# Two-layer fp32 trunk on one core: P.V key blocks in both column halves of TensorE, one-step pre-norm scaling, another order of attention steps

## The chip, the cores and the metric

One core of one Trainium2 chip runs the whole program in one launch. The metric is the device time of an execution in microseconds (us), and the kernel before is given as the median of three runs.

## The reference, cut to what matters

The trunk has two layers on 256 tokens of 1024 columns. Layer 0 is half SwiGLU, causal pooling mixer, half SwiGLU; layer 1 has sparse attention in the place of the pooling. Every sub-layer norms its input and its output.

```python
def rms_norm(x, g):
    y = xf * lax.rsqrt(jnp.mean(xf * xf, axis=-1, keepdims=True) + EPS)
    return (y * g.astype(jnp.float32)).astype(x.dtype)
...
    for i in range(DEPTH):
        g = norm_gains[i]
        f = swiglu(rms_norm(x, g[0]), ffn_w_gate[i, 0], ffn_w_up[i, 0], ffn_w_down[i, 0])
        x = x + 0.5 * rms_norm(f, g[1])
        h = rms_norm(x, g[2])
        m = pool_mixer(...) if i % N_MIXERS == 0 else nsa_mixer(...)
        x = x + rms_norm(m, g[3])
        f = swiglu(rms_norm(x, g[4]), ffn_w_gate[i, 1], ffn_w_up[i, 1], ffn_w_down[i, 1])
        x = x + 0.5 * rms_norm(f, g[5])
...
    # nsa_mixer: 16 heads in 4 key/value groups, head size 64
    o = gts[:, :, 0] * o_cmp + gts[:, :, 1] * o_sel + gts[:, :, 2] * o_win
    return o.reshape(B, S, Q_WIDTH) @ w_o
```

At 256 tokens the selected blocks and the window both cover all earlier keys, so the kernel computes the selected and the window branch as two dense causal branches of softmax(QK)V, and the compressed branch on 15 pooled keys.

## The kernel before, in words

Weights come from HBM in pieces of 128x1024 fp32 into a ring of four buffers (`raw`, issued by SP). ScalarE rounds each piece to fp32r (`hi`, the line `nc.scalar.activation(hi...)` in `pieces_of`), VectorE subtracts to get the rest (`lo`), and TensorE multiplies hi.hi, lo.hi and hi.lo into one sum (`mm3`). Tokens are worked in two tiles t of 128. An instruction scheduler orders the program for each engine; `urgent`, `after` and the attention's list `NSA_STEPS` guide it.

Between sub-layers, `post` adds the normed output to x, and `Pre.emit` makes the next input: `scaled` multiplies x by the gain (first 512 columns on POOL, L358, the others on VectorE, L359), `rstd` squares and sums x on ScalarE (L338), adds the halves on VectorE (`ms`, L341) and takes the power -0.5 on POOL (`rs`, L343). Where the input is normed at once, VectorE multiplies by that factor (L396, two halves), and TensorE transposes the result (L366). The pooling mixer applies the factor later.

In the attention, `qk(t, g)` makes the scores of a key/value group on TensorE (L850, L852), the row maximum on VectorE (L854), the exponentials on ScalarE (L856), the reciprocal and the gate product on VectorE (L861, L864), and POOL scales the weights (L865). `pv(t, g)` takes the key blocks (branch and key tile) in twos: TensorE transposes the weights of a block (L881), ScalarE copies the first block to SBUF and VectorE the second, and TensorE multiplies each by V in plain fp32 (L891). V has 64 columns, so the first block of the two uses the left half of TensorE's columns and the second the right half:

```python
nc.tensor.matmul(of32[i * HD:(i + 1) * HD], V[:, kt, br, g], PT[i], start=n == 0, stop=False)
```

The compressed branch adds two products with VC of 256 columns each, one in each half (L898). As both halves of the output are partial sums of the same four heads, ScalarE copies one (L909) and VectorE adds it to the other (L911) before the result is split in hi and lo. `cmp_mm` (L740) is the product of the compressed keys with its weights, also in both halves; `out_proj` is the last product of the attention, `wo` its weights.

Of the kernel before, what the change touches and what calls it, by code (L numbers as in the profile page):

```python
# [9 lines left out]
F32 = mybir.dt.float32  # L10
# [7 lines left out]
P = 128  # L18
# [20 lines left out]
    ("load", 1, 0),  # L39
    ("cpost", 0, 0),  # L40
    ("load", 1, 1),
    ("proj", 0, 1),
    ("load", 4, 0),
    ("proj", 1, 0),
    ("load", 4, 1),
    ("wcmp", 0, 0),
    ("proj", 4, 1),
    ("proj", 4, 0),
    ("load", 3, 0),
    ("cpost", 0, 1),  # L50
    ("proj", 1, 1),
    ("kpost", 0, 1),
    ("load", 3, 1),
    ("cmp", 0, 0),
    ("cpost", 1, 0),
    ("proj", 3, 0),
    ("hid", 0, 0),
    ("cpost", 1, 1),
    ("proj", 3, 1),
    ("kcmp", 0, 0),  # L60
    ("q", 0, 0),
    ("nope", 0, 0),
    ("wcmp", 1, 0),
    ("gates", 0, 0),
    ("vpost", 0, 1),
    ("load", 5, 0),
    ("cmp", 1, 0),
    ("q", 0, 1),
    ("load", 5, 1),
    ("vpost", 0, 0),  # L70
    ("rope", 0, 0),
    ("pc", 0, 0),
    ("proj", 5, 0),
    ("nope", 0, 1),
    ("hid", 1, 0),
    ("vcmp", 0, 0),
    ("pc", 0, 1),
    ("pct", 0, 0),
    ("rope", 0, 1),
    ("proj", 5, 1),  # L80
    ("q", 1, 0),
    ("qk", 0, 1),
    ("qk", 0, 0),
    ("nope", 1, 0),
    ("qk", 0, 1),
    ("qk", 0, 0),
    ("qk", 0, 0),
    ("q", 1, 1),
    ("pct", 0, 1),
    ("qk", 0, 0),  # L90
    ("nope", 1, 1),
    ("qk", 0, 1),
    ("rope", 1, 0),
    ("pv", 0, 0),
    ("qk", 0, 1),
    ("pv", 0, 0),
    ("pv", 0, 0),
    ("pc", 1, 0),
    ("qk", 1, 0),
    ("pv", 0, 1),  # L100
    ("pv", 0, 1),
    ("pv", 0, 1),
    ("vcmp", 1, 0),
    ("pct", 1, 0),
    ("qk", 1, 0),
    ("qk", 1, 0),
    ("qk", 1, 0),
    ("pv", 1, 0),
    ("pv", 1, 0),
    ("pv", 1, 0),  # L110
    ("pv", 1, 0),
    ("qk", 1, 1),
    ("qk", 1, 1),
    ("pv", 1, 0),
    ("rope", 1, 1),
    ("qk", 1, 1),
    ("qk", 1, 1),
    ("pv", 1, 1),
# [50 lines left out]
def _const_arrays():  # L169
# [14 lines left out]
    sel = np.repeat(np.eye(4, dtype=np.float32), P, axis=1)  # L184
# [8 lines left out]
    return np.ascontiguousarray(small), band, np.ascontiguousarray(sel)  # L193
# [13 lines left out]
def _layout(x, norm_gains, ffn_w_gate, ffn_w_up, ffn_w_down, pool_w, pool_b, pool_scale,  # L207
# [12 lines left out]
    a["pbs"] = np.ascontiguousarray(np.concatenate([pool_b[0].reshape(4, 256), pool_scale[0].reshape(4, 256)], axis=1))  # L220
# [13 lines left out]
    a["c_small"], a["c_band"], a["c_sel"] = _const_arrays()  # L234
# [4 lines left out]
def _trunk(ctx: ExitStack, tc: tile.TileContext, d, out):  # L239
# [44 lines left out]
    def piece(src, pool=None, tag="w", bufs=3, step=1024, cut=1024):  # L284
        return pieces_of(raw_piece(src, cut), pool, tag, bufs, step)

    def pieces_of(raw, pool=None, tag="w", bufs=3, step=1024):
# [35 lines left out]
    def halves(v):  # L323
        return [v[:, H[h]] for h in range(2)]
# [715 lines left out]
```

## Time and profile before

| | |
|---|---|
| median of 3 runs | 948.96 us (948.4 to 949.82) |
| the profiled execution's own time | 950.01 us |
| its span | 948.2 us |
| TensorE busy | 928.3 us, 98% of the span |
| VectorE, ScalarE, POOL busy | 655.1, 470.3, 78.8 us |

The span is the stretch from the first to the last instruction that the profiler saw; what the time has above it lies around the program. PE is TensorE, PEld its weight load, DVE VectorE, ACT ScalarE, SP the engine that issues the loads. A plain fp32 matmul leaves two records in the trace, an fp32r one leaves one. Records of matmuls overlap, so what one costs TensorE is read from its start to the start of the next.

### The profile page before, as it was taken

What the parts mean: (1) busy time and instruction counts of PE and PEld (TensorE: products, weight loads), DVE (VectorE), ACT (ScalarE), POOL (GpSimd) and SP (SyncE); (2) the same over time, 40 slices, a digit from 0 to 9 for tenths busy, and PEclk for the clock granted to TensorE, in tenths of its full rate; (3) what the DMA queues carried; (4) which work ended last, traced back from release to release, by engine and by line L of the source; (5) the groups of instructions that cost most, each with busy time, mean ns of one, the idle gap of its engine ahead of it and who ended that gap; (6) DMA issues with size and microseconds to landing.
All of it is one profiled execution on the core that took longest, in us unless ns stands there. A gap on an engine that the chain in (4) does not pass through costs nothing.

```text
span 948.2 us, 13030 instructions
## 1 busy us (share of the span) xinstructions
PE 928.3 (98%) x4882; PEld 769.6 (81%) x4882; DVE 655.1 (69%) x961; ACT 470.3 (50%) x800; POOL 78.8 (8%) x70
## 2 busy tenths in 40 slices
PE   8999999999999999999999999999999999999997
PEld 5888888877888888878888888888655678888886
DVE  6857577786967666658676676777974668676653
ACT  7644445355744344446444443546953566544421
POOL 1000001131000000120000002000542130000000
PEclk9999999999999999999999999999999999999999
DMA  8866675335866566248665652852200358665611
GB/s 321 288 206 199 213 239 196 116 107 168 281 218 220 180 195 205 89 148 279 218 208 190 200 182 78 315 200 90 90 0 24 110 179 285 207 217 182 196 45 44
DMA packets 48033, 168.96 MB, mean 178 GB/s; under 512 B 5593, under 2 KB 6105, under 8 KB 47970
## 3 DMA queue, kind: packets, MB, share of 16 engines
q1 hardware_dynamic: 47970, 168.13, 53.3%
q8 instruction: 38, 0.62, 0.3%
q14 instruction: 25, 0.20, 0.1%
HBM read 167.06 MB, written 1.05 MB: 177 GB/s over the span
## 4 chain that ended last, share of the span: by engine, by line
PE 51%; DVE 4%; ACT 2%; POOL 1%; issue 1%; DVEq 0%; POOLq 0%; ACTq 0%
PE g L503 14%; PE g L504 7%; PE acc L306 5%; PE acc L308 5%; PE acc L307 5%; PE g L306 3%; PE g L308 3%; PE g L307 3%; PE g L891 2%; PE g L881 1%; PE g L471 1%; POOL fx L358 1%; ACT big L856 1%; DVE ast L854 1%; DVE wlo L297 1%
## 5 line engine op out<-in xcount | busy, mean ns | idle before, releaser
L503 PE MATMUL g<-xT,whi 128*128 128x512 f32 x1152 | 406.0, 394 | 0.0
L504 PE MATMUL g<-xT,wlo 128*128 128x256 f32 x1152 | 325.1, 282 | 0.0
L296 ACT ACTIVATE whi<-raw 128x1024 fp32r<-128x1024 f32 (+2 forms) x252 | 205.1, 862 | 151.9 <-issue 48.3
L297 DVE TENSOR_TENSOR wlo<-raw,whi 128x1024 fp32r<-128x1024 f32 (+2 forms) x252 | 242.3, 1003 | 44.3 <-ACT whi L296 43.8
L503 PEld LDWEIGHTS g<-xT,whi 128*128 128x128 f32 x1152 | 216.3, 188 | 49.6
L504 PEld LDWEIGHTS g<-xT,wlo 128*128 128x128 f32 x1152 | 216.5, 188 | 1.4
L297 DVE TENSOR_TENSOR dlo<-raw,dhi 128x1024 fp32r<-128x1024 f32 (+1 forms) x128 | 119.2, 954 | 105.0 <-ACT dhi L296 104.7
L296 ACT ACTIVATE dhi<-raw 128x1024 fp32r<-128x1024 f32 (+1 forms) x128 | 103.8, 842 | 158.0 <-DMA raw<-in_wd 151.7
L440 DVE TENSOR_REDUCE sg<-g 128x256 f32<-128x512 f32 x144 | 97.8, 686 | 56.1 <-PE g L504 55.7
L306 PE MATMUL acc<-dhi,hTh 128*128 128x512 f32 x288 | 112.3, 390 | 0.0
L307 PE MATMUL acc<-dlo,hTh 128*128 128x512 f32 x288 | 112.0, 389 | 0.0
L308 PE MATMUL acc<-dhi,hTl 128*128 128x512 f32 x288 | 111.5, 389 | 0.0
L306 PE MATMUL g<-whi,xT 128*128 128x512 f32 (+2 forms) x168 | 63.9, 384 | 0.8 <-ACT xT L311 0.7
L307 PE MATMUL g<-wlo,xT 128*128 128x512 f32 (+2 forms) x168 | 63.8, 380 | 0.5 <-DVE wlo L297 0.5
L308 PE MATMUL g<-whi,xT 128*128 128x512 f32 (+2 forms) x168 | 63.5, 379 | 0.0
L343 POOL TENSOR_TENSOR rs<-ms,neghalf 128x1 f32<-128x1 f32 x24 | 13.6, 565 | 598.4 <-DVE ms L341 598.4
L306 PEld LDWEIGHTS acc<-dhi,hTh 128*128 128x128 f32 x288 | 54.1, 188 | 11.3
L308 PEld LDWEIGHTS acc<-dhi,hTl 128*128 128x128 f32 x288 | 54.0, 188 | 11.3
L307 PEld LDWEIGHTS acc<-dlo,hTh 128*128 128x128 f32 x288 | 54.1, 188 | 9.9
L306 PEld LDWEIGHTS g<-whi,xT 128*128 128x128 f32 x168 | 31.9, 191 | 7.5 <-ACT xT L311 2.0
L307 PEld LDWEIGHTS g<-wlo,xT 128*128 128x128 f32 x168 | 32.0, 190 | 7.1 <-DVE wlo L297 1.3
L308 PEld LDWEIGHTS g<-whi,xT 128*128 128x128 f32 x168 | 31.9, 190 | 6.4 <-DVE xT L312 0.7
(176 smaller groups left out, 991.4 us busy)
## 6 DMA issues: line engine op xcount, KB each, us to landing
raw<-in_wu SPq DMA_DIRECT2D x88, 512.0 KB, 4.6
raw<-in_wd SPq DMA_DIRECT2D x88, 512.0 KB, 4.5
raw<-in_wg SPq DMA_DIRECT2D x86, 512.0 KB, 3.9
raw<-in_win SPq DMA_DIRECT2D x18, 512.0 KB, 4.3
gain<-in_gains SPq DMA_DIRECT2D x11, 512.0 KB, 3.7
raw<-in_wo SPq DMA_DIRECT2D x8, 512.0 KB, 4.8
big<-in_wk SPq DMA_DIRECT2D x4, 512.0 KB, 5.9
big<-in_wv SPq DMA_DIRECT2D x4, 512.0 KB, 9.3
```

The costliest lines, as they stand in the source:

```text
L296: nc.scalar.activation(hi[:, n + a:n + b], r[:, a:b], AF.Copy)
L297: nc.vector.tensor_tensor(lo[:, n + a:n + b], r[:, a:b], hi[:, n + a:n + b].bitcast(F32), op=OP.subtract)
L306: nc.tensor.matmul(o, A[0], B[0], start=start, stop=False)
L307: nc.tensor.matmul(o, A[0], B[1], start=False, stop=False)
L308: return nc.tensor.matmul(o, A[1], B[0], start=False, stop=stop)
L343: nc.gpsimd.tensor_tensor(r, v, neghalf, op=OP.pow)
L358: nc.gpsimd.tensor_tensor(xg[:, H[0]], x[t][:, H[0]], g[:, H[0]], op=OP.mult)
L440: nc.vector.tensor_reduce(dst, o.rearrange("p a b -> p b a"), axis=AX.X, op=OP.add)
L471: nc.tensor.matmul(o, A(t, k)[i], B[k][j], start=n == 0, stop=n == len(its) - 1)
L503: nc.tensor.matmul(o, hi, pre.xx[:, :, k, :], start=k == 0, stop=False)
L504: nc.tensor.matmul(o[:, 1, :], lo, xT[0][:, k, :], start=False, stop=k == KD - 1)
L891: nc.tensor.matmul(of32[i * HD:(i + 1) * HD], V[:, kt, br, g], PT[i], start=n == 0, stop=False)
```

## The change: what it does

- `pv`: a key block is multiplied by V in two matmuls of 256 columns, one into each column half, as the compressed branch was. The halves of the output are then different heads, and the copy and the two adds (L909, L911) go.
- `Pre.emit`: a normed input takes x, the row's factor and the gain in one VectorE operation for each half. The pooling mixer's input takes its gain product on VectorE alone.
- The gate products (`ar`, `cst`), the scaling of the compressed weights (`ce`) and the `lo` part of the `wo` weights move from VectorE to POOL.
- The pooling's bias is one row of 1024 columns, added by 8 matmuls of 512 columns in the place of 16 of 256; its values come through two of the `raw` buffers.
- `NSA_STEPS` has the same kinds of steps in another order.

```diff
     def scaled(t, g):
         xg = fx[t]
-        nc.gpsimd.tensor_tensor(xg[:, H[0]], x[t][:, H[0]], g[:, H[0]], op=OP.mult)
-        nc.vector.tensor_mul(xg[:, H[1]], x[t][:, H[1]], g[:, H[1]])
+        for h in range(2):
+            nc.vector.tensor_mul(xg[:, H[h]], x[t][:, H[h]], g[:, H[h]])
...
+                elif self.normed:
+                    self.r[t] = r = rstd(halves(x[t]), False, t)
+                    xg = fx[t]
+                    for h in range(2):
+                        nc.vector.scalar_tensor_tensor(xg[:, H[h]], x[t][:, H[h]], r, self.g[:, H[h]], op0=OP.mult, op1=OP.mult)
                 else:
                     xg = scaled(t, self.g)
                     self.r[t] = r = rstd(halves(x[t]), False, t)
-                if self.normed and self.n:
-                    for h in range(2):
-                        nc.vector.tensor_scalar(xg[:, H[h]], xg[:, H[h]], r, None, op0=OP.mult)
...
+        for h in range(2):
+            bs = pp.tile([P, 1024], F32, name="raw", bufs=4)
+            nc.sync.dma_start(bs[0:1], d["pbs"][:, h * 1024:(h + 1) * 1024])
...
+            nc.gpsimd.tensor_tensor(bs[:, 0], bs[:, 0], bs[:, 1], op=OP.mult)
+            nc.gpsimd.tensor_copy(bias[0][:, H[h]], bs[:, 0])
+            nc.gpsimd.tensor_tensor(bias[1][:, H[h]], bs[:, 0], bias[0][:, H[h]].bitcast(F32), op=OP.subtract)
...
-                nc.vector.tensor_mul(st[:, 1], st[:, 1], gates[t][:, 8 * c:8 * c + 8])
-                nc.vector.tensor_mul(e, e, bc(st[:, 1]))
+                nc.gpsimd.tensor_tensor(st[:, 1], st[:, 1], gates[t][:, 8 * c:8 * c + 8], op=OP.mult)
+                nc.gpsimd.tensor_tensor(e, e, bc(st[:, 1]), op=OP.mult)
...
-                    nc.vector.tensor_mul(rv, rv, gv)
+                    nc.gpsimd.tensor_tensor(rv, rv, gv, op=OP.mult)
...
-                o = psG.tile([P, 2, 2, P], F32, name="g")
...
+                o = psG.tile([P, 2, P], F32, name="g")
+
+                def mm(A, B, start, stop):
+                    for par in range(2):
+                        nc.tensor.matmul(o[par * HD:(par + 1) * HD].rearrange("p b q -> p (b q)"), A,
+                                         B[:, par].rearrange("p b q -> p (b q)"), start=start, stop=stop)
...
-                        nc.tensor.matmul(of32[i * HD:(i + 1) * HD], V[:, kt, br, g], PT[i], start=n == 0, stop=False)
+                        mm(V[:, kt, br, g], qs_[i], n == i == 0, False)
...
-                for i in range(2):
-                    nc.tensor.matmul(o[i * HD:(i + 1) * HD, i].rearrange("p b q -> p (b q)"), VC[c],
-                                     q[:, i].rearrange("p b q -> p (b q)"), start=False, stop=True)
+                mm(VC[c], q, False, True)
...
-                ol = np_.tile([P, 512], F32, name="y", bufs=3)
-                of = np_.tile([P, 2, P], F32, name="of", bufs=1)
-                ol = ol[:HD].rearrange("p (a b q) -> p a b q", a=2, b=2)
-                nc.scalar.activation(ol, o[HD:], AF.Copy)
-                for par in range(2):
-                    nc.vector.tensor_tensor(of[par * HD:(par + 1) * HD], o[:HD, par], ol[:, par], op=OP.add)
-                split([v[:, 2 * g:2 * g + 2, :] for v in OT[t]], of)
+                split([v[:, 2 * g:2 * g + 2, :] for v in OT[t]], o)
...
-                    wo.append(ksplit(piece(d["wo"][:, i * 2048:(i + 1) * 2048], step=512), 2))
+                    wo.append(ksplit(piece(d["wo"][:, i * 2048:(i + 1) * 2048], step=512, eng=nc.gpsimd), 2))
```

Where the order of instructions moves, it is shown as the built programs have it. Line numbers of the change differ from those of before by a few. First TensorE in the middle of the attention: V products, transposes of weights (`big`) and of queries (`q`), and products with VC. Before:

```order
L798 MATMUL g<-csm,q_6161 128x128 x4
L891 MATMUL g<-PT,V 64x512
L798 MATMUL g<-csm,q_6161 128x128 x4
L891 MATMUL g<-PT,V 64x512
L881 MATMUL g<-csm,big 128x128 x4
L898 MATMUL g<-PT,VC_5108 64x256 x2
L881 MATMUL g<-csm,big 128x128 x4
```

The change, at the same place (L880 are the products with V and VC, L893 and L803 the transposes):

```order
L880 MATMUL g<-PT,V 64x256 x4
L893 MATMUL g<-csm,big 128x128 x8
L880 MATMUL g<-PT,VC_5094 64x256 x2
L803 MATMUL g<-csm,q_6163 128x128 x4
L880 MATMUL g<-PT,V 64x256 x2
L803 MATMUL g<-csm,q_6163 128x128 x4
L880 MATMUL g<-PT,V 64x256 x2
L774 MATMUL g<-wv_5088,rep 128x64 x2
L893 MATMUL g<-csm,big 128x128 x4
```

A V product of 512 columns often stands by itself before; in the change the two 256-column products of a block stand next to each other everywhere. Next POOL, from the second scaling of softmax weights on. Before, scalings follow each other:

```order
L343 TENSOR_TENSOR rs_5169<-ms_5167,neghalf 128x1
L865 TENSOR_TENSOR big<-big,ar 128x4x128 x4
L865 TENSOR_TENSOR big<-big,ar 128x1024
L895 TENSOR_TENSOR PT<-Pc,csm 128x512
L865 TENSOR_TENSOR big<-big,ar 128x1024
L895 TENSOR_TENSOR PT<-Pc,csm 128x512
```

The change (L870 are the scalings, L296 the `lo` parts of `wo`, L825 and L826 the compressed weights, L869 the gate products):

```order
L870 TENSOR_TENSOR big<-big,ar 128x4x128
L296 TENSOR_TENSOR wlo<-raw,whi 128x512
L825 TENSOR_TENSOR cst<-cst,gates_5079 128x8
L296 TENSOR_TENSOR wlo<-raw,whi 128x512 x3
L826 TENSOR_TENSOR ce<-ce,cst 128x128
L296 TENSOR_TENSOR wlo<-raw,whi 128x512 x4
L869 TENSOR_TENSOR ar<-ar,gates_5078 128x4
L870 TENSOR_TENSOR big<-big,ar 128x4x128
L869 TENSOR_TENSOR ar<-ar,gates_5079 128x4
L870 TENSOR_TENSOR big<-big,ar 128x1024
L906 TENSOR_TENSOR PT<-Pc,csm 128x512
```

Between the second and the third scaling now stand eight `wo` pieces and three small products. Last TensorE ahead of the attention, at `cmp_mm` of the compressed keys (the tile `big` here is its data; L696 and L707 are transposes). Before, its 32 matmuls stand in one row:

```order
L308 MATMUL g<-whi,xT 128x512
L696 MATMUL g<-csm,fx_70 128x128 x4
L740 MATMUL g<-big 64x128 x32
L707 MATMUL g<-csm,y 128x128 x4
L306 MATMUL g<-whi,xT 128x512
```

The change, where L745 is `cmp_mm` and L305 to L307 are the three products of `mm3`:

```order
L307 MATMUL g<-whi,xT 128x304
L745 MATMUL g<-big 64x128 x11
L305 MATMUL g<-whi,xT 128x512
L745 MATMUL g<-big 64x128 x8
L306 MATMUL g<-wlo,xT 128x512
L307 MATMUL g<-whi,xT 128x512
L305 MATMUL g<-whi,xT 128x512
L306 MATMUL g<-wlo,xT 128x512
L307 MATMUL g<-whi,xT 128x512
L305 MATMUL g<-whi,xT 128x512
L745 MATMUL g<-big 64x128 x4
```

The one row has become four, of 11, 8, 4 and (behind these) 9 matmuls, with other products between them.

## Rows read from the trace of the kernel before

**Rows 1.** The page's part 1: busy us (share of span) and instructions.

```profile
PE 928.3 (98%) x4882; PEld 769.6 (81%) x4882; DVE 655.1 (69%) x961; ACT 470.3 (50%) x800; POOL 78.8 (8%) x70
```

**Rows 2.** Part 4, the chain that ended last, by engine.

```profile
PE 51%; DVE 4%; ACT 2%; POOL 1%; issue 1%; DVEq 0%; POOLq 0%; ACTq 0%
```

**Rows 3.** Windows: stretch, length, busy PE, PEld, DVE, ACT, POOL; clock, DMA share, GB/s.

```profile
0.00:596.00 596.00, 590.30 (x3043) 499.63 (x3044) 417.75 (x546) 293.35 (x433) 34.92 (x38) 1.00 0.60 198
650.00:690.00 40.00, 36.65 (x216) 28.17 (x215) 35.29 (x105) 31.80 (x122) 15.49 (x12) 1.00 0.18 61
690.00:745.00 55.00, 53.82 (x247) 31.96 (x245) 30.09 (x65) 24.23 (x71) 18.79 (x15) 0.97 0.06 20
```

**Rows 4.** Timeline, PE: start, length, operation, records [idle before]; first and last lone V product.

```profile
677.01 1.07 PE L891 MATMUL g<-PT,V 128*64 128x512 f32 x2
...
734.98 1.07 PE L891 MATMUL g<-PT,V 128*64 128x512 f32 x2
735.98 0.50 PE L306 MATMUL acc<-whi,xT 128*128 128x512 f32 x1
```

**Rows 5.** Timeline, PE: two V products in a row; a VC pair and what follows.

```profile
711.43 1.08 PE L891 MATMUL g<-PT,V 128*64 128x512 f32 x4
712.34 0.60 PE L898 MATMUL g<-PT,VC 128*64 128x256 f32 x4
...
718.88 0.65 PE L898 MATMUL g<-PT,VC 128*64 128x256 f32 x4
719.46 0.66 PE L881 MATMUL g<-csm,big 128*128 128x128 f32 x4
```

**Rows 6.** Timeline, PE: waits in the attention and at its end.

```profile
689.02 0.33 PE L826 MATMUL g<-csm,ce 128*128 128x128 f32 x1 [1.83 <-DVE ce L821]
...
747.41 0.50 PE L306 MATMUL acc<-whi,ot 128*128 128x512 f32 x1 [1.11 <-ACT ot L311]
```

**Rows 7.** Windows of one us after those waits; the clock is the third last column.

```profile
691.00:692.00 1.00, 1.00 (x3) 0.29 (x2) 0.93 (x6) 0.35 (x2) 0.35 (x1) 0.50 0.00 0
```

**Rows 8.** Timeline, all engines, between the two FFNs: input of token tile 0.

```profile
394.43 1.69 POOL L358 TENSOR_TENSOR fx<-x,gain 128x512 f32<-128x512 f32 x1 [0.92 <-issue]
...
394.99 1.67 DVE L359 TENSOR_TENSOR fx<-x,gain 128x512 f32<-128x512 f32 x1
...
396.92 0.55 POOL L343 TENSOR_TENSOR rs<-ms,neghalf 128x1 f32<-128x1 f32 x1 [0.81 <-DVE ms L341]
...
398.14 0.63 PE L366 MATMUL g<-csm,fx 128*128 128x128 f32 x4 [0.18 <-DVE fx L396]
```

**Rows 9.** Timeline after the attention: input of token tile 1.

```profile
759.96 6.56 POOL L358 TENSOR_TENSOR fx<-x,gain 128x512 f32<-128x512 f32 x1 [1.31 <-DVE x L352]
...
765.28 0.21 DVE L341 TENSOR_SCALAR ms<-ssq 128x1 f32<-128x1 f32 x1
...
766.48 0.54 POOL L343 TENSOR_TENSOR rs<-ms,neghalf 128x1 f32<-128x1 f32 x1
...
767.69 1.07 PE L366 MATMUL g<-csm,fx 128*128 128x128 f32 x8 [1.34 <-DVE fx L396]
```

**Rows 10.** Timeline, PE: first input of the pooling mixer.

```profile
194.06 1.16 PE L366 MATMUL g<-csm,fx 128*128 128x128 f32 x7 [0.83 <-POOL fx L358]
```

**Rows 11.** Groups by shape: busy us, mean ns | idle before.

```profile
L389 DVE SCALAR_TENSOR_TENSOR fx<-x,rs,acc 128x512 f32<-128x512 f32 x4 | 2.8, 743 | 0.7 <-POOL rs L343 0.7
```

**Rows 12.** Timeline, POOL: the first scaling of softmax weights.

```profile
661.45 1.04 POOL L865 TENSOR_TENSOR big<-big,ar 128x512 f32<-128x512 f32 x1 [67.40 <-PE acc L852]
```

**Rows 13.** Timeline, PE: the first transposes of scaled weights.

```profile
674.29 0.60 PE L881 MATMUL g<-csm,big 128*128 128x128 f32 x4
```

**Rows 14.** Timeline, PE: one `cmp_mm` and what follows.

```profile
627.05 3.71 PE L740 MATMUL g<-big 128*64 128x128 f32 x64
630.70 0.55 PE L707 MATMUL g<-csm,y 128*128 128x128 f32 x3
```

**Rows 15.** The page's part 6: loads, KB each, median us to landing.

```profile
raw<-in_wu SPq DMA_DIRECT2D x88, 512.0 KB, 4.6
```

More of the change, by code (lines that the diff above doesn't have):

```diff
@@ L39 @@
     ("load", 1, 0),
+    ("wcmp", 0, 0),
+    ("load", 1, 1),
+    ("load", 4, 0),
     ("cpost", 0, 0),
-    ("load", 1, 1),
+    ("load", 4, 1),
+    ("load", 3, 0),
     ("proj", 0, 1),
-    ("load", 4, 0),
     ("proj", 1, 0),
-    ("load", 4, 1),
-    ("wcmp", 0, 0),
-    ("proj", 4, 1),
[L48 to L56, printed above, removed]
+    ("proj", 4, 0),
+    ("cpost", 0, 1),
+    ("load", 3, 1),
+    ("kpost", 0, 1),
+    ("proj", 1, 1),
+    ("cmp", 0, 0),
+    ("proj", 3, 0),
+    ("cpost", 1, 0),
+    ("cpost", 1, 1),
+    ("proj", 4, 1),
+    ("gates", 0, 0),
+    ("q", 0, 0),
+    ("load", 5, 0),
     ("hid", 0, 0),
-    ("cpost", 1, 1),
+    ("nope", 0, 0),
     ("proj", 3, 1),
+    ("wcmp", 1, 0),
+    ("vpost", 0, 1),
+    ("cmp", 1, 0),
     ("kcmp", 0, 0),
[L61 to L67, printed above, removed]
+    ("pc", 0, 0),
     ("q", 0, 1),
+    ("rope", 0, 0),
     ("load", 5, 1),
-    ("vpost", 0, 0),
-    ("rope", 0, 0),
-    ("pc", 0, 0),
     ("proj", 5, 0),
     ("nope", 0, 1),
+    ("qk", 0, 0),
     ("hid", 1, 0),
-    ("vcmp", 0, 0),
[L77 to L82, printed above, removed]
+    ("qk", 0, 0),
+    ("pc", 0, 1),
+    ("q", 1, 0),
+    ("pct", 0, 0),
+    ("proj", 5, 1),
+    ("qk", 0, 1),
+    ("rope", 0, 1),
+    ("qk", 0, 1),
+    ("vcmp", 0, 0),
     ("qk", 0, 0),
-    ("nope", 1, 0),
-    ("qk", 0, 1),
-    ("qk", 0, 0),
+    ("qk", 1, 1),
     ("qk", 0, 0),
     ("q", 1, 1),
+    ("qk", 1, 0),
+    ("nope", 1, 0),
     ("pct", 0, 1),
-    ("qk", 0, 0),
+    ("vpost", 0, 0),
+    ("pv", 0, 0),
     ("nope", 1, 1),
-    ("qk", 0, 1),
+    ("qk", 1, 0),
+    ("pc", 1, 0),
     ("rope", 1, 0),
     ("pv", 0, 0),
+    ("pv", 0, 0),
     ("qk", 0, 1),
-    ("pv", 0, 0),
-    ("pv", 0, 0),
-    ("pc", 1, 0),
+    ("pc", 1, 1),
+    ("qk", 0, 1),
+    ("pv", 0, 1),
+    ("pct", 1, 0),
     ("qk", 1, 0),
     ("pv", 0, 1),
[L101 to L106, printed above, removed]
+    ("qk", 0, 2),
     ("qk", 1, 0),
@@ L233, in _layout @@
     a["wo"] = _rows(nsa_w_o[0])
[L234 removed]
+    a["c_small"], a["c_band"] = _const_arrays()
     return a
@@ L608, in pooled @@
                 o = acc_tiles()
+                for h in range(2):
+                    for q in range(2):
+                        nc.tensor.matmul(o[h], on, bias[q][:, H[h]], start=q == 0, stop=False)
                 for g in range(4):
                     sl = slice(g * 256, (g + 1) * 256)
-                    mm = [(sel[:, g, :], bias[q]) for q in range(2)]
-                    mm += [(band[:, (t + b) * 4 + g, :], ys[b][q][:, sl]) for b in range(t + 1) for q in range(2)]
+                    mm = [(band[:, (t + b) * 4 + g, :], ys[b][q][:, sl]) for b in range(t + 1) for q in range(2)]
                     if t == 0:
@@ L615, in pooled @@
                     for n, (A, B) in enumerate(mm):
-                        nc.tensor.matmul(o[g // 2][:, g % 2 * 256:(g % 2 + 1) * 256], A, B, start=n == 0, stop=n == len(mm) - 1)
+                        nc.tensor.matmul(o[g // 2][:, g % 2 * 256:(g % 2 + 1) * 256], A, B, start=False, stop=g % 2 == 1 and n == len(mm) - 1)
                 return o
```

102 lines of the change are left out of this document (48 added, 54 removed).

## The prediction

> **What bounds the kernel now.** Part 1 of the page comes first: TensorE is busy 928.3 of 948.2 us [rows 1], no other engine above 69%. So the time goes where TensorE's work goes, and next to that where TensorE waits. The chain that ended last agrees: half of it is TensorE's own work, and other engines have only a few per cent each [rows 2]. I then read the windows by stage. Up to the attention TensorE idles 5.7 us in 596 [rows 3]. From 650 to 745 us, the stage that the change rewrites, it idles 3.35 + 1.18 = 4.5 us, while VectorE is busy 35.3 of the first 40 us. Last I read TensorE's own timeline there, from start to start, because the records overlap.
>
> **The V products.** A lone 512-column V product takes 735.98 - 734.98 = 1.00 us from its start to the next instruction's [rows 4]; 12 of the 24 stand so in TensorE's order, the first at 677.01, the last at 734.98. Two in a row, one in each column half, take 712.34 - 711.43 = 0.91 us for both [rows 5]: they run at the same time. A lone product thus leaves half of the columns unused. The new form is in the trace already: the two 256-column products with VC, one in each half, take 719.46 - 718.88 = 0.58 us as a pair, other work before and behind [rows 5]. I read a cost from these: going into and out of such a row costs 0.15 us, and each unit (256 columns in both halves, or half of a 512-column product) 0.43, since 0.15 + 0.43 = 0.58, 0.15 + 0.85 = 1.00, and 0.91 is two units with the way out still to come. In the orders both kernels have 22 such rows, so 0.15 x 22 stays. Units before: 24 for the 12 lone blocks, 22 for the other 12 blocks and the 8 VC products. After: 24 + 8 = 32. That is 14 x 0.43 = **6.0 us less**. The bounds are 0, if only the saved slots turn into waits, and a loss, if the halves do not overlap (rivals).
>
> **Input of the next sub-layer.** Before, POOL and VectorE multiply x by the gain, 1.69 and 1.67 us [rows 8], then VectorE scales by the factor. VectorE's product starts at 394.99 and ends half a microsecond after POOL's, so it got little done while POOL ran. The new operation, 0.74 us for a half, is in the trace [rows 11]. Where TensorE is covered by other products nothing is gained. Where it is not: 0.18 us before 398.14, where the power begins only at 396.92, behind the product [rows 8]; it goes wholly. The 0.83 us before 194.06 [rows 10] waits on POOL's product; VectorE alone does a half in about 0.7 but starts half a microsecond later, so I take 0.4, with bounds 0 and 0.83. Before 767.69, the sum of squares is done at 765.28 + 0.21 = 765.49, but the power waits until 766.48 behind POOL's 6.56 us product [rows 9]. Without it the power starts about 0.8 us sooner and the longer product gives back 0.1 to 0.3: I take 0.7 of the 1.34, bounds 0 and 1.34. Sum **1.3 us less**, between 0.2 and 2.4.
>
> **End of P.V.** The copy and two adds leave the way from the last VC product to `out_proj`; TensorE's wait there is 1.11 us before 747.41 [rows 6]. What goes is longer than the wait, so I take all of it: **1.1 us less**, and lower bound 0 if another operand is late next.
>
> **Compressed keys.** One row of `cmp_mm` takes 630.70 - 627.05 = 3.65 us for 32 matmuls in 16 pairs [rows 14]: 0.21 us a pair, and about 0.24 for going in and out. Split in four rows, it goes in and out three times more (0.7 us), and the odd rows of 11, 8 and 4 leave a pair broken three times (3 x 0.21 = 0.6). **1.3 us more**; 0 if the split fills a wait.
>
> **Work moved to POOL.** VectorE loses the 16 `lo` pieces of `wo`, the gate products and the adds, which relieves the one busy engine of the stage; POOL gains them. A piece has 512 columns as a scaling has, 1.04 us [rows 12]; the smallest products take at least what the power takes, 0.55 [rows 8]. Behind the second scaling stand now 8 pieces and 3 small products, 8 x 1.04 + 3 x 0.55 = 10.0 us, before the third scaling can start, and then a transpose and its V product wait for that. Before, the first scaling ended at 662.5 and its first reader started at 674.29, 11.8 us later [rows 12, 13]. So the queue just fits, and I take 0; if the pieces run at 1.69 as POOL's product did beside VectorE [rows 8], it is 8 x 0.65 = 5.2 longer, 3.4 us late. In the other direction, less work on VectorE may take up to half of the 4.5 us of waits. The Trainium skill ("SBUF — State Buffer", section "SBUF: two separate sides") says why a piece may stretch: POOL and a VectorE operation with two inputs from SBUF exclude each other for a whole instruction. By that rule the moved pieces are no free ride, they take turns with VectorE. The 1.67 us of VectorE's product beside POOL's agree [rows 8]; the rival "POOL late" below is what the rule would do at its worst here.
>
> **Half clock.** After waits of 1.83 us before 689.02 [rows 6] and another half microsecond, the granted clock is 0.50, that is 1.2 GHz, in the window at 691 [rows 7]; over 690 to 745 the mean is 0.97, so 0.03 x 55 = 1.7 us are lost. Whether the new order has such waits the trace cannot tell: I keep it, and put its going into a rival.
>
> **Bias.** The same columns in half as many matmuls: 0 on TensorE. Its values hold two of the four `raw` buffers for six POOL operations, at 1.04 to 1.69 us [rows 8, 12] 6 to 10 us. Two buffers bring 1 MB in some 4.6 us [rows 15] plus about 2.3 for hi and lo, 152 GB/s where the stage draws 198 [rows 3]. Over 10 us that is 2.3 us of weights short, hidden by pieces that are already converted, while TensorE has 590 of 596 us [rows 3]. I take 0, upper bound 2.3.
>
> **The sum.** 950.01 - 6.0 - 1.3 - 1.1 + 1.3 = 942.9 us. The profiled execution took 1.05 us more than the median of 948.96, so the forecast for the median is **941.9 us**. A change of 0.2%, 1.9 us, is about what a measurement of this kernel can tell from none: faster means below 947.1, slower above 950.9.
>
> **Rivals.** *More than that* (0.18): the half clock goes (1.7) and relief of VectorE takes half of the waits (2.2): 938.0. For it speaks that the wait before the drop is on VectorE's `ce` [rows 6], whose engine is relieved; against it, that `ce` now stands behind pieces on POOL. *The chain of softmax sets the end* (0.12): the V products get cheaper and TensorE waits for weights instead; then only the other terms stay, 950.01 - 1.3 - 1.1 + 1.3 - 1.05 = 947.9. For it speaks VectorE at 88% from 650 to 690 [rows 3]; against it, that TensorE idles just 1.2 us from 690 to 745, where most V products lie. *POOL late* (0.07): the queue of pieces falls behind VectorE. If two POOL operations stretch to the 6.56 us seen [rows 9], 2 x 5.5 = 11 us come on top: 952.9. It turns the sign from 9 us of new waits on. That 6.56 came while VectorE ran one product of two SBUF tensors after another; at the place of the pieces the order of the change gives VectorE mostly small operations. *The halves do not overlap* (0.03): each unit takes 0.85, 22 x 0.15 + 32 x 0.85 = 30.5 us instead of 3.3 + 46 x 0.43 = 23.1, and the time is 947.9 + 7.4 = 955.3. Against it stand the VC pairs, which are the same instruction on other data [rows 5].
>
> **Numbers.** The forecast has 0.60. The range from 936.0 to 947.9 takes in the forecast with its bounds (up to 3.4 late on POOL, 2.3 on `raw`), the rival below it and the softmax case; the forecast's own is 938 to 946. Faster: 0.60 + 0.18 and a quarter of the softmax case, 0.81; within 0.2%: the rest of it, 0.09; slower: 0.07 + 0.03 = 0.10.
>
> **What would show it.** Right: V products in pairs a few ns apart, one block 0.58 us from start to start and 0.43 behind another; TensorE's busy time about 6 us less from 650 to 745; no wait of 1.1 us at the first `out_proj` product after the last P.V; a power that starts right after the sum of squares at the last pre-norm. Wrong: transposes of weights that wait for POOL's scaling with `wo` pieces just ahead of it; idle time of TensorE above 10 us from 650 to 745; a half clock over a longer stretch; V products 0.85 us apart in a block.

## The result, and the profile after

The changed kernel takes **943.59 us** (943.27 to 944.33, 4 runs), the kernel before 949.19 us (948.4 to 949.82, 4 runs): ratio 0.9943, 95% interval 0.9925 to 0.996. The forecast was 941.9 with a range of 936.0 to 947.9. The profiled execution of the change took 944.33 us, with a span of 942.5; it lies 0.7 above the median, that of before 0.8 (1.05 above the median of three runs from which the forecast started). Each ratio further down is to the kernel before as it ran beside that run, where its median was 948.64 to 950.56 us; so of two runs the one with the lower time can have the higher ratio.

Parts 1 and 4 of the page of the changed kernel, to set beside [rows 1, 2]:

```profile
PE 922.8 (98%) x4922; PEld 771.4 (82%) x4922; DVE 634.5 (67%) x899; ACT 466.2 (49%) x792; POOL 84.3 (9%) x104
...
PE 94%; DVE 3%; ACT 2%; issue 1%; DMA 0%; POOL 0%; DVEq 0%; POOLq 0%; SPq 0%; ACTq 0%
```

The 94% is not to be set against the 51% of [rows 2]. The shares of before add up to 59%, since that chain was followed back only to 393.5 us; of what it covers TensorE has 51 of 59, that is 86%, and not the half that the prediction read.

TensorE's busy time fell by 928.3 - 922.8 = 5.5 us. Its idle time, span less busy, is 942.5 - 922.8 = 19.7 where it was 948.2 - 928.3 = 19.9. So nearly the whole gain is work, and the 2.4 us of waits that were to go came back in other places. The windows say where (columns as in [rows 3]; the order of steps is another, so that the stretches hold only roughly the same work):

```profile
0.00:596.00 596.00, 590.16 (x3039) 498.92 (x3040) 414.59 (x542) 293.93 (x434) 23.48 (x34) 1.00 0.60 199
650.00:690.00 40.00, 34.26 (x205) 29.68 (x206) 28.29 (x71) 25.75 (x95) 23.69 (x30) 0.91 0.26 80
690.00:745.00 55.00, 54.17 (x328) 36.56 (x327) 27.52 (x60) 29.13 (x97) 31.88 (x35) 1.00 0.12 39
```

From 690 to 745 TensorE hardly waits and runs at full clock. From 650 to 690 it idles 5.7 us where it idled 3.35, and the mean clock is 0.91: 0.09 x 40 = 3.6 us lost at half clock, against 1.7 before. VectorE is less busy there (28.3 for 35.3), and yet it is what TensorE ends up waiting for.

TensorE's waits of the attention, longest first (what waited, for what: us in total, times, longest):

```profile
PE acc L855 <- ACT big L861: 3.6, 1, 3.6
PE g L814 <- DVE kbd L766: 1.4, 1, 1.4
PE g L789 <- ACT y L783: 0.7, 1, 0.7
```

The 3.6 us is one wait. The timelines of POOL, VectorE, ScalarE and TensorE around it (start, length, engine, operation, records, [idle before]):

```profile
671.81 5.08 POOL L296 TENSOR_TENSOR wlo<-raw,whi 128x512 fp32r<-128x512 f32 x4
...
670.05 1.53 DVE L772 COPY rep<-hidT 128x128 f32<-128x128 f32 x2
671.86 1.33 DVE L688 TENSOR_TENSOR y<-rB,rA 128x64 f32<-128x64 f32 x1
673.22 1.27 DVE L685 TENSOR_TENSOR rA<-rV,csm 128x128 f32<-128x128 f32 x1
674.42 1.35 DVE L686 TENSOR_TENSOR rB<-rV,csm 128x128 f32<-128x128 f32 x1
675.69 1.27 DVE L859 TENSOR_REDUCE ast<-acc 128x2 f32<-128x512 f32 x2
...
676.40 0.47 ACT L861 ACTIVATE big<-acc,ast 128x256 f32<-128x256 f32 x1 [2.55 <-DVE ast L859]
...
677.48 0.39 PE L855 MATMUL acc<-kTh,q 128*128 128x256 f32 x1 [3.64 <-ACT big L861]
```

Read it from the bottom. The score product L855 waits for a free accumulator, which ScalarE's exponential L861 frees. That waits for the row maxima L859 of VectorE, and they stand behind three small products of RoPE that take 1.3 us each, as long as one of the four pieces of `wo` that POOL makes meanwhile (5.08 / 4 = 1.27). In the kernel before such products took 0.21 to 0.29, but for one of 0.73. The reductions L859 read PSUM and are not stretched: 1.27 for two. The three products together take 3.95 us where some 0.8 would do, so the maxima come about 3 us late. Soon after the wait the clock is at half, for 6.8 us in all where the kernel before has 3.4 (windows of 1 us; the clock is the third last column):

```profile
679.00:680.00 1.00, 0.95 (x4) 0.65 (x4) 1.00 (x4) 1.00 (x4) 0.00 (x0) 0.50 0.60 242
684.00:685.00 1.00, 1.00 (x6) 0.90 (x6) 0.62 (x2) 1.00 (x5) 1.00 (x1) 0.50 0.00 0
```

The other places of the prediction, on TensorE's timeline of the changed kernel; one V product with V and one with VC in a row, the first input of the pooling mixer, the input that is new among the waits, the input of token tile 0 between the FFNs, and the first product after P.V:

```profile
704.15 0.65 PE L880 MATMUL g<-PT,V 128*64 128x256 f32 x4
704.73 0.65 PE L893 MATMUL g<-csm,big 128*128 128x128 f32 x4
...
740.07 0.65 PE L880 MATMUL g<-PT,V 128*64 128x256 f32 x4
740.55 0.60 PE L880 MATMUL g<-PT,VC 128*64 128x256 f32 x4
741.08 0.65 PE L893 MATMUL g<-csm,big 128*128 128x128 f32 x4
...
194.27 0.90 PE L365 MATMUL g<-csm,fx 128*128 128x128 f32 x5 [0.40 <-DVE fx L358]
...
213.38 0.44 PE L365 MATMUL g<-csm,fx 128*128 128x128 f32 x2 [1.51 <-DVE fx L394]
...
397.61 1.12 PE L365 MATMUL g<-csm,fx 128*128 128x128 f32 x7
...
742.78 0.50 PE L305 MATMUL acc<-whi,ot 128*128 128x512 f32 x1 [0.47 <-ACT ot L310]
```

A lone block takes 704.73 - 704.15 = 0.58 us where it took 1.00 [rows 4], and two in a row 741.08 - 740.07 = 1.01, so 0.43 for the second. The waits of 0.83 [rows 10] and 0.18 [rows 8] are 0.40 and nothing, that of 1.11 [rows 6] is 0.47. A wait of 1.51 before 213.38 is new.

### The profile page after: what moved, and what is told of

It is laid out like the page before. It is cut to its first block, busy times and chain, and to the rows that moved or that the text cites. A ratio compares the mean times of both kernels' runs of the same rounds, so it can differ in the third digit from the quotient of the medians.

```text
span 942.5 us, 13047 instructions
## 1 busy us (share of the span) xinstructions
PE 922.8 (98%) x4922; PEld 771.4 (82%) x4922; DVE 634.5 (67%) x899; ACT 466.2 (49%) x792; POOL 84.3 (9%) x104
## 3 DMA queue, kind: packets, MB, share of 16 engines
HBM read 167.05 MB, written 1.05 MB: 178 GB/s over the span
## 4 chain that ended last, share of the span: by engine, by line
PE 94%; DVE 3%; ACT 2%; issue 1%; DMA 0%; POOL 0%; DVEq 0%; POOLq 0%; SPq 0%; ACTq 0%
PE g L504 28%; PE g L505 15%; PE acc L305 9%; PE acc L307 9%; PE acc L306 9%; PE g L305 5%; PE g L306 5%; PE g L307 5%; PE g L472 2%; PE g L365 1%; PE g L880 1%; PE g L893 1%; PE g L745 1%; PE acc L855 1%; ACT big L861 1%
## 5 line engine op out<-in xcount | busy, mean ns | idle before, releaser
L296 DVE TENSOR_TENSOR wlo<-raw,whi 128x1024 fp32r<-128x1024 f32 (+2 forms) x236 | 230.8, 1020 | 47.5 <-ACT whi L295 47.1
L296 DVE TENSOR_TENSOR dlo<-raw,dhi 128x1024 fp32r<-128x1024 f32 (+1 forms) x128 | 119.4, 954 | 95.3 <-ACT dhi L295 95.2
L305 PE MATMUL acc<-dhi,hTh 128*128 128x512 f32 x288 | 112.3, 390 | 0.0
L307 PE MATMUL acc<-dhi,hTl 128*128 128x512 f32 x288 | 111.5, 389 | 0.0
L305 PE MATMUL g<-whi,xT 128*128 128x512 f32 (+2 forms) x168 | 65.1, 388 | 0.8 <-ACT xT L310 0.8
L307 PE MATMUL g<-whi,xT 128*128 128x512 f32 (+2 forms) x168 | 63.5, 380 | 0.0
L307 PEld LDWEIGHTS acc<-dhi,hTl 128*128 128x128 f32 x288 | 54.1, 188 | 11.2
L305 PEld LDWEIGHTS acc<-dhi,hTh 128*128 128x128 f32 x288 | 54.0, 188 | 11.3
L310 ACT ACTIVATE hTh<-sg 128x512 fp32r<-128x512 f32 x36 | 22.3, 619 | 34.1 <-DVE sg L444 34.1
L305 PEld LDWEIGHTS g<-whi,xT 128*128 128x128 f32 x168 | 32.2, 192 | 7.8 <-ACT xT L310 1.9
```

Source lines behind the costliest of these rows:

```text
L296: (eng or nc.vector).tensor_tensor(lo[:, n + a:n + b], r[:, a:b], hi[:, n + a:n + b].bitcast(F32), op=OP.subtract)
L305: nc.tensor.matmul(o, A[0], B[0], start=start, stop=False)
L307: return nc.tensor.matmul(o, A[1], B[0], start=False, stop=stop)
L310: return (nc.scalar.activation(dst[0], src, AF.Copy), nc.vector.tensor_tensor(dst[1], src, dst[0].bitcast(F32), op=OP.subtract))
```

## The experiments

Theory 1, formed on these rows: the pieces of `wo` on POOL block VectorE's operations, and what was forecast as 0 costs some 4 us in waits and clock; without them the change gives what its other parts promise. Theory 2, its rival: the other order of steps put the operations of the attention where they wait, and the pieces only stand beside them.

**Pieces of `wo` back on VectorE** in the changed kernel.

```diff
-                    wo.append(ksplit(piece(d["wo"][:, i * 2048:(i + 1) * 2048], step=512, eng=nc.gpsimd), 2))
+                    wo.append(ksplit(piece(d["wo"][:, i * 2048:(i + 1) * 2048], step=512), 2))
```

> The change with the lo parts of wo back on VectorE, nothing else. Theory 1 (the pieces on POOL and VectorE's operations with two SBUF inputs take turns, VectorE's small operations stretch from 0.2-0.3 to 1.3 us, the row maxima come late, TensorE waits 3.64 us and falls to half clock for 6.8 us): the stretched operations, the 3.6 us wait and most of the half clock (3.4 us) go: 937 to 940. Theory 2 (the V products got cheaper and the softmax chain itself sets the end): VectorE has 16 x 0.69 = 11 us more to do, the waits stay or grow: 943 to 946.

Measured: 940.07 us (939.91 to 940.3, 4 runs), ratio to the kernel before 0.9892 (0.9875 to 0.9909), wholly below that of the change. Part 1, the window of the attention's first part and VectorE's operations there:

```profile
PE 920.6 (98%) x4922; PEld 769.0 (82%) x4922; DVE 640.0 (68%) x915; ACT 465.7 (50%) x792; POOL 65.9 (7%) x88
...
650.00:690.00 40.00, 36.93 (x241) 30.89 (x242) 33.10 (x91) 29.97 (x116) 17.53 (x24) 1.00 0.23 76
...
670.35 0.35 DVE L772 COPY rep<-hidT 128x128 f32<-128x128 f32 x2
671.35 0.22 DVE L688 TENSOR_TENSOR y<-rB,rA 128x64 f32<-128x64 f32 x1
672.09 1.28 DVE L859 TENSOR_REDUCE ast<-acc 128x2 f32<-128x512 f32 x2
673.37 0.26 DVE L685 TENSOR_TENSOR rA<-rV,csm 128x128 f32<-128x128 f32 x1
```

The same operations take 0.22 and 0.26, the two copies 0.35 for 1.53, the reductions as before. No wait of TensorE in the attention is above 1.1 us, and the clock stays whole up to the last matmul. The span is 942.5 - 938.1 = 4.4 us shorter: busy time 922.8 - 920.6 = 2.2 (half clock), idle time 19.7 - 17.5 = 2.2. Theory 1, in its size too. Against the kernel before, busy time is 7.7 us less and idle time 2.4. That this is the prediction's sum of waits, 1.3 + 1.1, is chance: the wait of 1.83 for `ce` [rows 6] is gone too, which the sum had not, and the new wait of 1.5 at 213 us is still there.

**The pieces on POOL in the kernel before**, alone: the lower of the two lines turned into the upper one, nothing else.

> The kernel before with the lo pieces of wo on POOL, alone. Theory 1 (a long POOL operation with two inputs from SBUF blocks VectorE's operations of that kind, in whatever order of steps): new waits of TensorE of 3 us or more between 660 and 700 us, the half clock longer than the 3.4 us of before, and the median 952 to 956 where the kernel before has 949 to 950. Theory 2 (the pieces hurt only in the order of steps of the change, and VectorE at 88 per cent gains from the relief): 947 to 950.

Measured: 956.24 us (953.95 to 958.07, 8 runs), ratio 1.0049 (1.0029 to 1.0069). VectorE's timeline and a new wait of TensorE:

```profile
650.68 1.32 DVE L678 COPY rV<-y 128x128 f32<-128x128 f32 x1
652.03 1.25 DVE L681 TENSOR_TENSOR rB<-rV,csm 128x128 f32<-128x128 f32 x1
...
654.03 1.06 PE L798 MATMUL g<-csm,q 128*128 128x128 f32 x8 [2.17 <-DVE rA L748]
```

Theory 1, just above its range: the same stretch in the old order of steps. Two things that it named did not come. No wait between 660 and 700 us reaches 3 us (the longest are 1.92 and 1.53), though idle time is 955.6 - 931.4 = 24.2 us in all for 19.9. And the longer half clock is not in the attention: in this profile it came from 206 to 213 us, at the pooling mixer, where nothing was changed, and once more behind the attention, at 762, where TensorE had waited 2.55 us. Runs of this kernel with a mean clock of 0.996 to 0.997 took 954.0 to 954.2, and runs of before with 0.997 to 0.999 took 948.5 to 950.6, so between runs of a like clock the pieces cost 3.4 to 5.7 us.

**The pieces cut in 256 columns** on POOL (in 128 in a further run), otherwise the change.

```diff
-                    wo.append(ksplit(piece(d["wo"][:, i * 2048:(i + 1) * 2048], step=512, eng=nc.gpsimd), 2))
+                    wo.append(ksplit(piece(d["wo"][:, i * 2048:(i + 1) * 2048], step=256, eng=nc.gpsimd), 2))
```

> The changed kernel with the pieces of wo cut in 256 columns in place of 512 (twice as many operations on ScalarE and POOL, each half as long; the work is the same). Theory 1 (VectorE's operations wait for the end of one whole POOL operation): the small VectorE operations of 0.2 to 0.3 us that took 1.3 us beside the pieces take 0.6 to 0.8 us, TensorE's wait of 3.64 us before L855 falls to 1.5 to 2.5, the half clock shrinks, and the median is 940 to 942.5. Theory 2 (VectorE is only slowed by how much POOL does in all, or waits for something else at that place): the stall stays near 3.6 us and the median is 943 to 945, or later since there are more operations.

Measured: 939.08 us (939.0 to 940.33, 4 runs), ratio 0.9873 (0.985 to 0.9896), below the expected range of theory 1 and far from theory 2. The same VectorE operations, and POOL's:

```profile
670.72 0.77 DVE L688 TENSOR_TENSOR y<-rB,rA 128x64 f32<-128x64 f32 x1
671.53 0.40 DVE L685 TENSOR_TENSOR rA<-rV,csm 128x128 f32<-128x128 f32 x1
671.85 0.82 DVE L686 TENSOR_TENSOR rB<-rV,csm 128x128 f32<-128x128 f32 x1
...
671.72 4.79 POOL L296 TENSOR_TENSOR wlo<-raw,whi 128x256 fp32r<-128x256 f32 x6
```

POOL does more in all (32 pieces in 24.1 us for 16 in 20.3), and VectorE is held less: 0.8 us, again the length of one piece (4.79 / 6 = 0.80). The wait before L855 is 0.77 at most (1.6 in three waits), and the half clock is gone from the attention. So it is the length of one POOL operation that counts here, not POOL's load. The cut makes ScalarE's rounding of these pieces shorter too; what that does by itself, no run shows.

> The changed kernel with the pieces of wo cut in 128 columns on POOL (64 operations in place of 16). Theory 1 (a VectorE operation waits for one POOL operation, so the block gets shorter with the piece): the small VectorE operations stretch to at most 0.6 us, no wait of TensorE over 1 us between 650 and 745, and the median is 938 to 940, level with the cut at 256. Theory 2 (what each operation costs besides its columns counts by now): POOL's time for the pieces grows from 24.1 to 32 us or more, scalings start late, and the median is above 941.

Measured: 942.77 us (942.33 to 944.22, 4 runs), ratio 0.9933 (0.9917 to 0.995). The stretch went as theory 1 says (L688 0.44 and 0.49), the time as theory 2. POOL needs 27.7 us for the 64 pieces, less than the 32 expected. Its span is 942.4 - 937.2 = 5.2 us longer than with 256 columns. Of that, 1.5 lie before the attention, where this profile has half clock after the wait of 1.51 us at 213 (from there to the next inputs at 227.41 it takes 14.1 us, with 256 columns 12.6). In the attention TensorE waits 0.9 us for POOL's scaling, 1.3 for ScalarE's copy of weights and 0.8 for VectorE. The half clock is not the reason: another run, with a mean clock of 1.0, took 942.7. How much is POOL's queue, I have not settled.

**Small products.** First all that moved to POOL in the attention back on VectorE:

```diff
-                nc.gpsimd.tensor_tensor(st[:, 1], st[:, 1], gates[t][:, 8 * c:8 * c + 8], op=OP.mult)
-                nc.gpsimd.tensor_tensor(e, e, bc(st[:, 1]), op=OP.mult)
+                nc.vector.tensor_mul(st[:, 1], st[:, 1], gates[t][:, 8 * c:8 * c + 8])
+                nc.vector.tensor_mul(e, e, bc(st[:, 1]))
...
-                    nc.gpsimd.tensor_tensor(rv, rv, gv, op=OP.mult)
+                    nc.vector.tensor_mul(rv, rv, gv)
...
-                    wo.append(ksplit(piece(d["wo"][:, i * 2048:(i + 1) * 2048], step=512, eng=nc.gpsimd), 2))
+                    wo.append(ksplit(piece(d["wo"][:, i * 2048:(i + 1) * 2048], step=512), 2))
```

> The changed kernel with all that moved to POOL in the attention back on VectorE: the lo pieces of wo and the small gate products. Theory 1 (only the long pieces hurt; the small products take 0.20 to 0.24 us on POOL and are neither gain nor loss): within 1 us of the run with the pieces alone back, that is 939 to 941. Theory 2 (VectorE needs the relief from the small products): 941.5 to 943.5. Theory 3 (the round trip through POOL costs something for each gate product): below 939.

Measured: 940.43 us (939.94 to 941.37 in four runs; a fifth took 2338.87, and nothing shows why), ratio 0.9884 (0.9861 to 0.9908): level with the run that moved the pieces alone. Theory 1. Then the small products on VectorE with the pieces in 256 columns on POOL:

> The pieces of wo in 256 columns on POOL, and the small gate products back on VectorE. If the small products wait behind pieces on POOL and the round trip costs time, 937.5 to 939; if VectorE needs that relief, 940 to 942; if neither, 939 to 940, as with the cut alone.

Measured: 944.05 us (943.59 to 945.87, 4 runs), ratio 0.9952 (0.9937 to 0.9967), slower than any case that I had named. Its POOL timeline:

```profile
666.91 11.76 POOL L296 TENSOR_TENSOR wlo<-raw,whi 128x256 fp32r<-128x256 f32 x16
678.64 1.04 POOL L870 TENSOR_TENSOR big<-big,ar 128x512 f32<-128x512 f32 x1
```

Without the small products between them, the pieces stand 16 in a row for 11.8 us, where the change has rows of 4 at most; the third scaling starts only at 678.64 behind them. TensorE's longest wait is 2.8 us, before 680.01, for `ce` of VectorE, whose products take 0.7 to 1.1 us there, and the clock is at half from 679 to 686. Whether the late scaling or the held VectorE counts for more, this run doesn't part. Half clock behind the wait at 213 us came in this profile too, as in the run with 128 columns.

**The order of steps.** The table of before in the changed kernel, first with the pieces on POOL, then with them on VectorE.

```diff
 NSA_STEPS = [
     ("kpost", 0, 0),
     ("load", 1, 0),
-    ("wcmp", 0, 0),
-    ("load", 1, 1),
-    ("load", 4, 0),
     ("cpost", 0, 0),
+    ("load", 1, 1),
...
```

> The change with the list of attention steps of before. If the new order causes the waits: under 941. If the pieces on POOL cause them (theory 1): the order hardly matters, 942 to 946.

Measured: 945.36 us (942.15 to 946.83, 5 runs), ratio 0.9938 (0.9916 to 0.996): theory 1. TensorE's longest wait in the attention is 2.16 us here, before 648.98, for `rA` of VectorE.

> The changed kernel with the pieces of wo back on VectorE and the order of steps of before. It asks what the new order is worth when the pieces are out of the way. Theory 1 (the order is worth nothing by itself): 939.5 to 941.5, as with the new order. Theory 2 (the new order was needed to place the P.V steps): 943 or more, with new waits of TensorE between 650 and 745 us.

Measured: 940.14 us (939.49 to 942.65, 4 runs), ratio 0.9912 (0.9895 to 0.993), with the pieces on VectorE and the new order 940.07. One new wait of TensorE is there, 1.43 us before 679.83, and 3.4 us of half clock follow it. By the times the order brings and costs nothing that can be measured in either setting, and theory 2 falls, this run's and the rival of the whole section: with the old order the pieces cost 945.36 - 940.14 = 5.2 us, with the new one 943.59 - 940.07 = 3.5.

**The V products**, alone in the kernel before, and taken out of the change (the two forms of `pv` in the diff ahead of the prediction, exchanged as a whole).

> The kernel before with the new P.V alone. Theory 1: the 6.5 us of V products and up to 1.1 us of the end of P.V. come through: 941.5 to 943. Theory 2: TensorE waits for the weights instead, VectorE is at 88% there: 946 to 949.

Measured: 941.64 us (940.6 to 942.6, 4 runs), ratio 0.9908 (0.9889 to 0.9927): theory 1. Part 1:

```profile
PE 920.2 (98%) x4930; PEld 770.1 (82%) x4930; DVE 648.8 (69%) x945; ACT 465.9 (50%) x792; POOL 76.4 (8%) x70
```

TensorE's busy time is 8.1 us less than in [rows 1]. Summed over all V and VC products from start to next start, less waits, they take 24.8 us in the kernel before, 17.7 here. 1.4 us of those 24.8 are half clock: the row at 690.75, in the stretch of [rows 7], takes 2.40 us, and a pair of blocks at full clock 0.91 [rows 5] to 1.0. This kernel has no half clock before its last matmul; its longest wait in the attention is 1.99 us, before 740.22, for VectorE's copy of weights. By the medians this one edit gives more than the whole change; the intervals of the two ratios just touch.

> The change with the P.V of before. Theory 1: 6 to 7.5 us come back, 949.5 to 951. Theory 2: the waits shrink by what the V products take, 944 to 946.

Measured: 948.86 us (948.25 to 950.48, 10 runs), ratio 0.9988 (0.9976 to 1.0): 5.3 us above the change, just under the range of theory 1. Here the products of the old form take only 19.3 us, in 17 rows for the 22 of before, since the new order happens to put more of them in pairs. So order and edit reach partly for the same gain, and only 1.9 of the 4.2 us by which the span is longer than the change's are busy time. The other 2.3 are waits that come back with the old P.V, among them 0.7 for its adds, 0.5 more before `out_proj` (0.99 for 0.47) and 0.9 at the last pre-norm.

**The pre-norm**, alone in the kernel before, then taken out of the kernel with pieces of 256 columns (the edits of `scaled` and `emit` in the diff, made and unmade).

> The kernel before with the one-step scaling of the pre-norms alone (row factor and weights in one VectorE operation of 0.74 us a half, no product on POOL). Theory 1 (the prediction's term of 1.3 us is real): TensorE's wait before 194.06 falls from 0.83 to about 0.4, the one of 0.18 before 398.14 is gone, and the one of 1.34 before 767.69 falls below 0.7; the span is 1 to 2.4 us shorter and the median 947.5 to 949 where the kernel before has 949 to 950. Theory 2 (what is gained at the head of a sub-layer is given back by weights that are not there sooner): the three waits fall and others grow by as much, and the time is within 0.5 us of the kernel before.

Measured: 950.17 us (949.6 to 951.48, 12 runs), ratio 0.9991 (0.9978 to 1.0003). Two waits fell as forecast, 0.41 for 0.83 and none for 0.18; the third is 0.81 for 1.34, not below 0.7. And TensorE now waits for the input of the FFN behind the pooling mixer. First the kernel before there, then this one:

```profile
213.42 1.04 PE L366 MATMUL g<-csm,fx 128*128 128x128 f32 x8
...
214.34 1.32 PE L366 MATMUL g<-csm,fx 128*128 128x128 f32 x8 [0.90 <-DVE fx L395]
```

The time is that of theory 2.

> The pieces of wo in 256 columns on POOL, with the pre-norms of the kernel before (product by the weights on POOL and VectorE, then a scaling by the row factor). Theory 1 (the one-step scaling saves TensorE's waits that were counted in the prediction, 1.3 us): 940 to 941.5, where the same kernel with the one-step scaling has 939.08; TensorE waits 0.8 us before 194 again, and over 0.5 near 757. Theory 2 (its gain is given back elsewhere): 938.6 to 939.6.

Measured: 938.62 us (938.33 to 940.24, 4 runs), ratio 0.9895 (0.988 to 0.991), against 939.08 with the one-step scaling: theory 2. TensorE's timeline at that input with the old scaling, where L365 doesn't wait:

```profile
211.81 1.04 PE L365 MATMUL g<-csm,fx 128*128 128x128 f32 x8
213.30 0.96 PE L470 MATMUL g<-whi,xT 128*128 128x512 f32 x3 [0.45 <-ACT xT L310]
```

The first product of that FFN starts here at 213.30, and at 214.91 in the kernel before. From the first input of the mixer (194.22 and 194.06) that is 19.08 us for 20.85, with the old scaling in both: 0.33 of the difference is a wait that has gone, and 1.4 is less work, all of it in the bias, which takes half as many matmuls, and in the band products that alternate with it. With the one-step scaling this start is at 214.56, and the gain is gone.

One forecast of this run failed: near 757 us, at the last pre-norm, TensorE does not wait with the old scaling either. In the kernel before with the new P.V alone, which has the old scaling too, that wait is also gone; in the change with the old P.V it is back (0.9 us). So what took it away in the change is the new P.V, and not the scaling. The input of token tile 1 in this run, and with the new P.V alone:

```profile
755.64 1.06 PE L365 MATMUL g<-csm,fx 128*128 128x128 f32 x8
...
758.14 1.06 PE L366 MATMUL g<-csm,fx 128*128 128x128 f32 x8
```

## Why the prediction was right, and where it was not

The time lies 1.7 us above the forecast (944.33 for 942.9 in the profiles), and the sign and the main term hold. That it came so close is in part luck. The pieces on POOL, put at 0, cost 4.4 us of span. Without them the change takes 939.91 in its profile, 3.0 less than the terms add up to: the half clock of before (1.7) and the wait of 1.83 for `ce` are gone and `cmp_mm` cost 0.6 less than said, against which stand new waits of up to 1.1 in the attention and of 1.5 at 213.

- **V products, 6.0 us less.** Right in mechanism and size. After the change the 22 rows take 17.2 us, where the count of rows and units gave 17.1. Before, they took 24.8, of which 1.4 is the half clock in one row, so 23.4 at full clock where the count gave 23.1. The term is 6.2, and a run of its own shows it.
- **End of P.V, 1.1 less.** The wait went from 1.11 to 0.47: 0.6. The way that the prediction saw was not the one that TensorE waited for. ScalarE in the kernel before:

```profile
745.39 1.66 ACT L296 ACTIVATE whi<-raw 128x512 fp32r<-128x512 f32 x3
...
746.95 0.40 ACT L311 ACTIVATE ot<-of 128x256 fp32r<-128x256 f32 x1
747.38 0.60 ACT L909 ACTIVATE y<-g 64x512 f32<-64x512 f32 x1
```

TensorE waits for the split at 746.95. Its sums were done by VectorE at 743.16 + 0.85 = 744.01, so it stood behind weights that ScalarE rounds; the copy of the last VC product starts at 747.38, when the wait is nearly over. In the change TensorE waits for such a split still. How much of the 0.6 is the missing copies and how much the order, no run parts; with the old P.V put back the wait is 0.99, and there a copy does stand before the split.
- **Compressed keys, 1.3 more.** One of the two is split, in rows of 11, 8, 4 and 9 matmuls with two records each:

```profile
618.76 1.52 PE L745 MATMUL g<-big 128*64 128x128 f32 x22
620.64 1.09 PE L745 MATMUL g<-big 128*64 128x128 f32 x16
623.27 0.66 PE L745 MATMUL g<-big 128*64 128x128 f32 x8
625.20 1.31 PE L745 MATMUL g<-big 128*64 128x128 f32 x18
```

The products behind them start at 620.22, 621.67, 623.85 and 626.44, so the four rows take 4.31 us where one row took 3.65: 0.66, half of the term. Within a row a pair starts 0.218 us after the pair before it; 16 x 0.218 leaves about 0.15 of the 3.65 for going in and out, not 0.24. And rows of 8 and 4 break no pair; those of 11 and 9 end on a lone matmul each, which makes one pair more, not three: 17 x 0.218 + 4 x 0.15 = 4.31.
- **Pre-norm, 1.3 less, and bias, 0.** The first two waits that were named fell as said, by 0.43 and 0.18. The last is gone, but by the new P.V; the scaling alone took 0.53 of its 1.34. What the prediction missed is a fourth place, the input of the FFN behind the pooling mixer, to which TensorE came without a wait at 213.42 before and for which it waits 1.51 before 213.38 now. VectorE there, in the change:

```profile
211.97 0.69 DVE L349 TENSOR_TENSOR fx<-acc,gain 128x512 f32<-128x512 f32 x1 [0.92 <-ACT junk L337]
212.58 1.40 DVE L394 SCALAR_TENSOR_TENSOR fx<-x,rs,gain 128x512 f32<-128x512 f32 x2
```

The bias edit is worth 1.4 us of TensorE's work ahead of it, not 0. It brings TensorE there sooner, and the one-step scaling, all of it behind the row factor and here behind a product of the other tile too (211.97), comes no sooner. Up to the input at 596 us both edits together bring 0.28 (596.14 before, 595.86 now); the norm alone gains nothing that can be measured, in either kernel.
- **Work moved to POOL, 0.** This step failed. The queue was counted, and it did fit: the third scaling starts at 677.41 and no transpose waits for it. What was not counted is VectorE on the other side of the turn-taking. The prediction had the rule, and took it as a threat to POOL ("POOL late") alone, with the argument that VectorE has mostly small operations at that place. A small operation that must wait for a whole POOL operation is no small operation: 0.22 to 0.28 became 1.3. The price is 2.2 us of waits and about as much of clock in the profiles, 3.5 us by the medians.
- **Half clock, kept.** It doubled with the pieces (3.6 us lost for 1.7), which is the prediction's own sign of being wrong, "a half clock over a longer stretch". In the new order it is gone when the pieces are on VectorE or cut in 256 columns (but not with 16 of them in a row), so there it belongs to the step above. With the pieces on VectorE and the old order, 3.4 us of half clock stay, as many as before.

The Trainium skill ("SBUF — State Buffer", section "SBUF: two separate sides") says that a GpSimd operation and a VectorE operation that reads two inputs from SBUF, or runs in a two-port mode, hold a shared port for a whole instruction; it names fp32 copies within SBUF as such a mode. The traces agree: products of two SBUF tensors and copies took up to 1.3 us beside pieces of 1.3 and up to 0.8 beside pieces of 0.80, and reductions that read PSUM kept their 0.65 to 0.69. Of the rivals, "more than that" (938.0) is near to what the change does once the pieces are off POOL or cut.

The best kernels run are the change with pieces of 256 columns (939.08, ratio 0.9873), with the old pre-norm too (938.62, ratio 0.9895), and with the pieces on VectorE (940.07, ratio 0.9892). The intervals of their ratios overlap; all three lie below that of the change.

## What to carry to other kernels

Before moving work to POOL, count not only whether POOL's queue has room, but which VectorE operations stand beside it: each one that reads SBUF twice, or copies within SBUF, can take as long as the POOL operation, and what stands behind it on VectorE is late by the sum. If work goes there, cut it short, though not at any price: here 256 columns brought 4.5 us, and 128 lost 3.7 of them again. Sixteen pieces in a row took 944.05; that something of the critical chain should stand between pieces is likely from this, but not shown. And when a term makes TensorE arrive sooner at a place, ask at that place what it will now wait for: a gain of 1.4 us went unseen into a wait of 1.51.

## What was not expected of the hardware

- A wait of some 2 us can cost as much again in clock (before: 1.83 and 0.52 of waits, 1.7 lost), and not each time. The kernel with the old order of steps took 945.4 to 946.8 us in runs with a mean clock of 0.991 to 0.996, and 942.2 to 942.4 in runs with 0.999. The wait of 1.51 us at 213 us was followed by half clock in two of the nine profiles that have it, and by full clock in the others. In the kernel before with the pieces on POOL the clock fell at 206 us with no wait over 0.4 us in the ten us ahead of it. What decides it, the runs here don't show.
- A piece of 512, 256 and 128 columns takes POOL 1.30, 0.79 and 0.47 us, turns with VectorE included: a quarter of the columns costs more than a third of the time.
- The smallest products (128 x 4 and 128 x 8) take POOL 0.20 us, at the median of the changed kernel, and 0.56 at most, not the 0.55 that was worked from the power.
- Which side waits is not fixed. Beside VectorE's row of products at 760 us in the kernel before, POOL's product took 6.56 us [rows 9] and VectorE's kept 0.68 or 0.69 each; beside POOL's rows of pieces it is VectorE's products that take 1.3.
